# Two heads' products in a fixed order, another emission pace, and neighbourhood scores that no longer wait for the values

## The chip, the cores and the metric

The kernel runs on one core of one Trainium2 chip. The metric is device time in microseconds (us), from the start to the end of the one launch. The five engines of the core are written as in the profile: PE (TensorE, matrix products; PEld is its weight load), DVE (VectorE), ACT (ScalarE), POOL (GpSimd, which here only issues transfers) and SP (SyncE, transfers too).

## The reference, cut to what matters

A trunk of two layers over 512 tokens of width 1024. Each layer is a half-step feed-forward block, a mixer, and a second half-step feed-forward block; a last RMSNorm closes the trunk.

```python
x = x + 0.5 * swiglu(rmsnorm(x, ffn1_norm), ffn1_wg, ffn1_wu, ffn1_wd)
h = rmsnorm(x, mix_norm)
proj = h @ w_in            # q, k, v of 8 neighbourhood heads; q, k, v, gate, codes of 4 GLA heads
na_o  = rmsnorm(neighbourhood_attention(q, k, v, rpb), na_gain)
o_fwd = gla_chunked(qg, kg, vg, log_gf, True)
o_bwd = flip(gla_chunked(flip(qg), flip(kg), flip(vg), flip(log_gb), False))
gla_o = rmsnorm(o_fwd + o_bwd, gla_gain) * silu(g_r)
x = x + concatenate([na_o, gla_o], axis=-1) @ w_out
x = x + 0.5 * swiglu(rmsnorm(x, ffn2_norm), ffn2_wg, ffn2_wu, ffn2_wd)
```

Only the mixer is touched by the change. Everything is in float32.

## The kernel before

**Products.** A large product is done in three passes (`mm3`, L168): each operand is split into a high part and a rest (`split`, L147: ACT writes the high part, DVE the rest), and high*high, high*rest, rest*high are summed in PSUM. The weights arrive by DMA, are split into tiles `wh` and `wl` (six buffers each), and PE takes 512 columns a time. The small products of the attention are plain float32; the trace shows each of them as two records.

**The mixer** (`mixer`, L533) has four streams of work:

- `fillers` (L930) walks through `PAIRS`: eleven pairs of 128-wide column blocks of the input projection, one after the other. A pair takes 48 products of 512 columns (96 of 256 for the values `v`), and its `post` writes the scaled result. After the last pair come the output projection's products over the four neighbourhood head pairs (`op_part(c, 0, 4)`), which the generator emits once the neighbourhood part is normalised, then those over the gated linear attention (GLA) heads.
- `na_all` (L901) runs eight units (`na_unit`, L842), each half the queries of two heads: scores (L853), softmax (L860 to L871), transposes (L876), products with the values (L887). Three units are in flight, at different ages.
- `gla_all(0)`, `gla_all(1)` (L970) each treat two GLA heads: decay factors, then scores by levels of a binary tree of block sizes. Eight sets of 64x64 blocks (`blocks`, L624), one of 128x128 blocks (L701), two of 128x256 (L715), and at last `gla_out` (L753), which sums the products with the values.

The two heads of a unit lie in SBUF rows 0 to 63 and 64 to 127, so their score products use different halves of PE's rows; the two heads' products with the values use different halves of its columns. The kernel emits head 0, head 1, head 0, head 1.

**What sets the order.** `interleave` (L505) decides in which order the four streams emit. Each stream yields pairs (time its work takes, time until it should go on); the stream that is ready emits. `LVL` is the pause of a GLA stream after a level's DVE work, `NAP` the length of a neighbourhood unit, `OUTT` the time booked for a `gla_out`. A stream that yields a name waits until that result exists in `got`. The emission order is then handed to the tile framework, which makes each engine's final order from it by its own estimate of times, subject to the data and to the buffers. On the chip each engine takes its instructions in that final order.

**Buffers.** PSUM has eight banks: four `mm` (projections, GLA outputs, output projection), two `sc` (all scores, always taken as a pair), one `tp` (transposes and norm sums), one `o` (products of the neighbourhood heads with the values). So only one set of scores exists at a time, and the next waits until DVE or ACT has read the one before.

**Names.** The trace and the orders cut buffer numbers or layer digits from names: `M_mm` a projection or output product, `M_sc` scores, `M_tp` a transpose, `M_o` products with the values, `M_pp` the probabilities, `M_ga` and `M_kt` the GLA operands, `M_at`, `M_am`, `M_af` GLA score matrices, `M_vt` scaled GLA values before their transposes, `M_gv` after, `M_nacc` the sum of squares of the neighbourhood output, `M_oh` split outputs, `M_r` a reciprocal root.

Of the kernel before, what the change touches and what calls it, by code (L numbers as in the profile page):

```python
# [15 lines left out]
P = 128  # L16
# [8 lines left out]
LVL = 8.71  # L25
# [8 lines left out]
NAP = 10.4  # L34
# [24 lines left out]
OUTT = 8.24  # L59
# [4 lines left out]
def trunk_kernel(ctx, tc, xin, wgu, wdn, win, wcode, wgate, wout, vec, rpbt,  # L64
# [102 lines left out]

    def mm3(ps, wh, wl, rh, rl, first, last, more=False):  # L168
        PE.matmul(ps, wh, rh, start=first, stop=False, skip_group_check=more)  # L169
        PE.matmul(ps, wh, rl, start=False, stop=False, skip_group_check=more)  # L170
        PE.matmul(ps, wl, rh, start=False, stop=last, skip_group_check=more)  # L171

# [360 lines left out]
    def mixer(l):  # L533
        st["lab"] = f"M{l}"
        got = {}
# [63 lines left out]
        def gla_levels(pr):  # L599
# [24 lines left out]
            def blocks(pss, op):  # L624


                for i in range(8):
                    o = (i % 2) * 64
                    for hh in range(2):
                        PE.matmul(pss[hh][o:o + 64, (i // 2) * 64:(i // 2 + 1) * 64], *op(hh, i),  # L630
                                  start=True, stop=True)
# [17 lines left out]
            for li, h in enumerate((1, 2, 4, 8, 16, 32, 64, 128)):  # L649
# [45 lines left out]
                elif h2 == 128:  # L695
                    pss = psum("sc"), psum("sc")
                    for s in range(4):
                        t = s ^ 1
                        kk, qq = (KF, QF) if s < t else (KB, QB)
                        for hh in range(2):  # L700
                            PE.matmul(pss[hh][:, s * P:(s + 1) * P], kk[rows[hh], s * P:(s + 1) * P],  # L701
                                      qq[rows[hh], t * P:(t + 1) * P], start=True, stop=True)
# [4 lines left out]
                else:  # L707
                    for half in range(2):
# [3 lines left out]
                        for j in range(2):  # L712
                            s = 2 * half + j
                            for hh in range(2):
                                PE.matmul(pss[hh][:, j * 256:(j + 1) * 256],  # L715
                                          kk[rows[hh], s * P:(s + 1) * P], qq[rows[hh], o:o + 256],
                                          start=True, stop=True)
# [124 lines left out]
        def na_unit(hp, jp, pps, ctxd):  # L842
# [4 lines left out]
            for jj in range(2):  # L847
                j = 2 * jp + jj
                for hh in range(2):
                    kb = k[rows[hh], :]  # L850
                    krhs = bass.AP(kb.tensor, kb.offset + KOFF[j][0],
                                   [list(kb.ap[0]), [64, 2], [KOFF[j][1], 2], [1, 64]])
                    PE.matmul(sco[hh][:, jj * 256:(jj + 1) * 256], q[rows[hh], j * P:(j + 1) * P], krhs,  # L853
                              start=True, stop=True)
# [24 lines left out]
            if jp == 0:  # L879
                ctxd["po"] = psum("o")  # L880
            po = ctxd["po"]
            for jj in range(2):
                j = 2 * jp + jj
                for c in range(2):
                    v = got["v", hp][VSEL[j][c]]
                    for hh in range(2):
                        PE.matmul(po[rows[hh], j * P:(j + 1) * P], v[:, rows[hh]],  # L887
                                  pps[hh][:, (jj * 2 + c) * P:(jj * 2 + c + 1) * P],
                                  start=(c == 0), stop=(c == 1))
# [11 lines left out]
        def na_all():  # L901
# [4 lines left out]
            for u in range(8 + DEEP):  # L906
                if u < 8:
                    yield ("qk", u // 2)
                    yield ("v", u // 2)
                    units.append(na_unit(u // 2, u % 2, pps, ctxd))  # L910
                left = NAP if u < 8 else 3.0
                for age, n in enumerate((1, 2, 1)):
                    if 0 <= u - age < 8:
                        for _ in range(n):
                            y = next(units[u - age])
                            left -= sum(y)
                            yield y
# [233 lines left out]
```

## Time and profile before

| | us |
|---|---|
| median of 3 runs (lowest to highest) | 1954.99 (1954.86 to 1955.47) |
| the profiled execution | 1957.23 |
| its span, first to last instruction | 1955.5 |
| layer 0: start of the mixer to the start of the attention | 361.5 to 386.0 |
| layer 0: attention beside the projections | 386.0 to 548.7 |
| layer 0: attention after the last projection product | 548.7 to 562.8 |
| layer 0: GLA outputs and most of the output projection | 562.8 to 617.1 |
| layer 0: rest of the output projection | 617.1 to 634.4 |
| layer 1: the same mixer | 1328.5 to 1597.4 |

The rest of the span is the four feed-forward blocks. The profile page gives busy time for each engine, the chain of work that ended last, and groups of equal instructions. The mean granted clock of TensorE is 0.991 of full speed over the span. A table by stretches gives busy time and granted clock of each stage; the timeline gives start and length of single instructions. Products overlap in PE's pipeline, so the length of one record is longer than the time to the next; what a product costs is read from start to start.

### The profile page before, as it was taken

What the parts mean: (1) busy time and instruction counts of PE and PEld (TensorE: products, weight loads), DVE (VectorE), ACT (ScalarE), POOL (GpSimd) and SP (SyncE); (2) the same over time, 40 slices, a digit from 0 to 9 for tenths busy, and PEclk for the clock granted to TensorE, in tenths of its full rate; (3) what the DMA queues carried; (4) which work ended last, traced back from release to release, by engine and by line L of the source; (5) the groups of instructions that cost most, each with busy time, mean ns of one, the idle gap of its engine ahead of it and who ended that gap; (6) DMA issues with size and microseconds to landing.
All of it is one profiled execution on the core that took longest, in us unless ns stands there. A gap on an engine that the chain in (4) does not pass through costs nothing.

```text
span 1955.5 us, 32220 instructions
## 1 busy us (share of the span) xinstructions
PE 1924.7 (98%) x12490; PEld 1687.4 (86%) x12490; DVE 1416.9 (72%) x2705; ACT 1020.1 (52%) x1959; POOL 17.4 (1%) x36
## 2 busy tenths in 40 slices
PE   8999999999998999999999999999999999999997
PEld 7889989888777898999889899988887778999896
DVE  6958768676558875967788596776764689679585
ACT  5535536465564553644555364455654655546364
POOL 0000000000000000000000000000000000000000
PEclk9999999999999999999999999999999899999999
DMA  4333223322202332332223333232221033233322
GB/s 154 112 108 108 89 106 124 110 67 98 66 31 85 102 108 89 106 108 103 83 98 106 108 109 107 88 119 96 96 86 55 21 120 107 89 107 109 108 76 76
DMA packets 58249, 187.78 MB, mean 96 GB/s; under 512 B 6640, under 2 KB 13296, under 8 KB 45808
## 3 DMA queue, kind: packets, MB, share of 16 engines
q1 hardware_dynamic: 29904, 132.07, 19.8%
q10 hardware_dynamic: 25632, 45.27, 7.0%
q0 software_dynamic: 2560, 8.39, 1.3%
q8 instruction: 98, 1.61, 0.3%
q14 instruction: 55, 0.45, 0.1%
HBM read 183.60 MB, written 2.10 MB: 95 GB/s over the span
## 4 chain that ended last, share of the span: by engine, by line
PE 97%; DVE 1%; DMA 1%; ACT 1%; issue 0%; DVEq 0%; ACTq 0%
PE F_mm L169 14%; PE F_mm L171 14%; PE F_mm L170 14%; PE F_sc L169 9%; PE F_sc L170 9%; PE F_sc L171 9%; PE M_mm L169 6%; PE M_mm L170 6%; PE M_mm L171 6%; PE M_o L887 1%; PE M_sc L630 1%; PE M_tp L876 1%; PE M_sc L853 1%; PE M_mm L773 1%; PE M_sc L715 1%; DMA wraw<-in_wgu 0%
## 5 line engine op out<-in xcount | busy, mean ns | idle before, releaser
L149 ACT ACTIVATE F_wh<-F_wraw 128x512 fp32r<-128x512 f32 (+1 forms) x472 | 289.5, 617 | 439.9 <-PE F_sc L170 238.8
L169 PE MATMUL F_mm<-F_xc,F_wh 128*128 128x256 f32 x1792 | 500.5, 282 | 1.3 <-ACT F_wh L149 1.3
L170 PE MATMUL F_mm<-F_xc,F_wh 128*128 128x256 f32 x1792 | 501.5, 282 | 0.0
L171 PE MATMUL F_mm<-F_xc,F_wl 128*128 128x256 f32 x1792 | 495.2, 282 | 0.0
L150 DVE TENSOR_TENSOR F_wl<-F_wraw,F_wh 128x512 fp32r<-128x512 f32 (+1 forms) x472 | 312.8, 668 | 151.9 <-ACT F_wh L149 143.4
L169 PEld LDWEIGHTS F_mm<-F_xc,F_wh 128*128 128x128 f32 x1792 | 339.3, 190 | 3.7 <-ACT F_wh L149 1.9
L170 PEld LDWEIGHTS F_mm<-F_xc,F_wh 128*128 128x128 f32 x1792 | 340.3, 190 | 1.9
L171 PEld LDWEIGHTS F_mm<-F_xc,F_wl 128*128 128x128 f32 x1792 | 335.8, 190 | 0.0
L169 PE MATMUL F_sc<-F_hid,F_wh 128*128 128x512 f32 (+1 forms) x716 | 275.6, 387 | 1.3 <-DVE xt L455 1.3
L170 PE MATMUL F_sc<-F_hid,F_wh 128*128 128x512 f32 (+1 forms) x716 | 276.6, 386 | 0.0
L171 PE MATMUL F_sc<-F_hid,F_wl 128*128 128x512 f32 (+1 forms) x716 | 276.4, 386 | 0.0
L149 ACT ACTIVATE F_wh<-F_ws 128x512 fp32r<-128x512 f32 x256 | 161.8, 632 | 170.0 <-PE F_mm L170 109.8
L150 DVE TENSOR_TENSOR F_wl<-F_ws,F_wh 128x512 fp32r<-128x512 f32 x256 | 174.8, 688 | 41.8 <-ACT F_wh L149 38.8
L169 PEld LDWEIGHTS F_sc<-F_hid,F_wh 128*128 128x128 f32 x716 | 134.6, 188 | 29.0 <-DVE xt L455 3.0
L171 PEld LDWEIGHTS F_sc<-F_hid,F_wl 128*128 128x128 f32 x716 | 134.5, 188 | 26.4
L170 PEld LDWEIGHTS F_sc<-F_hid,F_wh 128*128 128x128 f32 x716 | 134.6, 188 | 25.7
L455 DVE SCALAR_TENSOR_TENSOR xt<-F_sc,xt 128x512 f32<-128x512 f32 x94 | 65.0, 691 | 96.7 <-PE F_sc L171 96.1
L169 PE MATMUL M_mm<-F_xd,M_wh 128*128 128x512 f32 x304 | 122.1, 403 | 0.0
L171 PE MATMUL M_mm<-F_xd,M_wl 128*128 128x512 f32 x304 | 120.3, 397 | 0.0
L170 PE MATMUL M_mm<-F_xd,M_wh 128*128 128x512 f32 x304 | 119.9, 395 | 0.0
L150 DVE TENSOR_TENSOR M_wl<-M_wraw,M_wh 128x512 fp32r<-128x512 f32 (+1 forms) x112 | 73.4, 669 | 35.9 <-ACT M_wh L149 32.4
L149 ACT ACTIVATE M_wh<-M_wraw 128x512 fp32r<-128x512 f32 (+1 forms) x112 | 67.6, 614 | 46.8 <-PE M_mm L170 37.9
(325 smaller groups left out, 3153.0 us busy)
## 6 DMA issues: line engine op xcount, KB each, us to landing
F_wraw<-in_wgu SPq DMA_DIRECT2D x64, 1024.0 KB, 4.7
F_wraw<-in_wdn SPq DMA_DIRECT2D x32, 1024.0 KB, 4.9
M_wraw<-in_win ACTq DMA_DIRECT2D x88, 256.0 KB, 3.6
F_wraw<-in_wgu ACTq DMA_DIRECT2D x80, 256.0 KB, 3.8
F_wraw<-in_wdn SPq DMA_DIRECT2D x16, 768.0 KB, 4.3
M_pp<-in_rpbt POOLq DMA_DIRECT2D x32, 256.0 KB, 3.1
M_wraw<-in_wout SPq DMA_DIRECT2D x16, 256.0 KB, 2.7
xt<-in_xin SPq DMA_DIRECT2D x8, 256.0 KB, 5.2
```

Source lines behind the costliest of these rows:

```text
L149: S.activation(h, src, AF.Copy)
L150: V.tensor_tensor(l, src, h.bitcast(F32), op=ALU.subtract)
L169: PE.matmul(ps, wh, rh, start=first, stop=False, skip_group_check=more)
L170: PE.matmul(ps, wh, rl, start=False, stop=False, skip_group_check=more)
L171: PE.matmul(ps, wl, rh, start=False, stop=last, skip_group_check=more)
L455: V.scalar_tensor_tensor(xt[:, c, :], pss[j], 0.5, xt[:, c, :], ALU.mult, ALU.add)
L630: PE.matmul(pss[hh][o:o + 64, (i // 2) * 64:(i // 2 + 1) * 64], *op(hh, i), start=True, stop=True)
L715: PE.matmul(pss[hh][:, j * 256:(j + 1) * 256], kk[rows[hh], s * P:(s + 1) * P], qq[rows[hh], o:o + 256], start=True, stop=True)
L773: PE.matmul(dst, vs(2 * half + j), fa[:, o:o + P], start=False, stop=(j == 1))
L853: PE.matmul(sco[hh][:, jj * 256:(jj + 1) * 256], q[rows[hh], j * P:(j + 1) * P], krhs, start=True, stop=True)
L876: PE.transpose(pt[:, i * P:(i + 1) * P], pp[:, i * P:(i + 1) * P], idn)
L887: PE.matmul(po[rows[hh], j * P:(j + 1) * P], v[:, rows[hh]], pps[hh][:, (jj * 2 + c) * P:(jj * 2 + c + 1) * P], start=(c == 0), stop=(c == 1))
```

## The change

**The head pairs.** A new helper `paired` takes a list of products and emits them in that order; all but the first of a list are told to stay in program order. Five places use it: the 64x64, 128x128 and 128x256 scores of the GLA streams, and the scores and the products with the values of the neighbourhood units. Within a pair head 1 now comes before head 0. The number, shape and operands of the products are the same.

**The pace.** `LVL` goes from 8.71 to 5.0, `NAP` from 10.4 to 8.0, `OUTT` from 8.24 to 3.6.

**The wait for the values.** A neighbourhood unit used to be created when both its queries and keys (`qk`) and its values (`v`) existed. Now it starts with `qk` alone, and the stream waits for `v` only before the products with the values.

```diff
-LVL = 8.71
+LVL = 5.0
-NAP = 10.4
+NAP = 8.0
-OUTT = 8.24
+OUTT = 3.6
...
+    def paired(mms):
+
+        for i, (ps, lhs, rhs, kw) in enumerate(mms):
+            ins = PE.matmul(ps, lhs, rhs, **kw)
+            if i:
+                tc.keep_in_program_order(ins)
+
...
-                for i in range(8):
-                    o = (i % 2) * 64
-                    for hh in range(2):
-                        PE.matmul(pss[hh][o:o + 64, (i // 2) * 64:(i // 2 + 1) * 64], *op(hh, i),
-                                  start=True, stop=True)
+                paired([(pss[hh][i % 2 * 64:i % 2 * 64 + 64, (i // 2) * 64:(i // 2 + 1) * 64], *op(hh, i), SS)
+                        for i in range(8) for hh in (1, 0)])
...
             if jp == 0:
+                yield ("v", hp)
                 ctxd["po"] = psum("o")
...
             for u in range(8 + DEEP):
                 if u < 8:
                     yield ("qk", u // 2)
-                    yield ("v", u // 2)
                     units.append(na_unit(u // 2, u % 2, pps, ctxd))
...
                             y = next(units[u - age])
+                            if isinstance(y[0], str):
+                                yield y
+                                y = next(units[u - age])
```

The final order of every engine in both mixers differs from the one before; the feed-forward blocks keep theirs but for a few rows at the start of the second one. In layer 0 (layer 1 has the same order in both versions) these are the places to know. In the orders of the changed kernel the products of `paired` stand under its line, L171, and the three passes of `mm3` under L176 to L178.

*Place 1: PE, the first set of 128x256 scores of a GLA stream, before.*

```order
L170 MATMUL M_mm_5645<-F_xd_3834,M_wh_5667 128x512
L715 MATMUL M_sc_5529<-M_ga_4147 128x256 x2
L171 MATMUL M_mm_5645<-F_xd_3834,M_wl_5668 128x512
L715 MATMUL M_sc_5530<-M_ga_4147 128x256 x2
L169 MATMUL M_mm_5800<-F_xd_3605,M_wh_5802 128x512
```

*The second set of the same stream in the changed kernel:*

```order
L176 MATMUL M_mm_5729<-F_xd_3681,M_wh_5761 128x512
L171 MATMUL M_sc_5268<-M_ga_4165 128x256
L177 MATMUL M_mm_5729<-F_xd_3681,M_wh_5761 128x512
L171 MATMUL M_sc_5267<-M_ga_4165 128x256
L171 MATMUL M_sc_5268<-M_ga_4165 128x256
L171 MATMUL M_sc_5267<-M_ga_4165 128x256
L178 MATMUL M_mm_5729<-F_xd_3681,M_wl_5762 128x512
```

Before, both products of head 0 (`M_sc_5529`) stand together, and those of head 1 behind a projection product. Now the heads alternate, but the first product, which is not held in order, stands alone ahead of a projection product.

*Place 2: PE at the last projection product of the mixer, before.* `M_mm_5800` and `M_mm_5801` are the last projection pair.

```order
L170 MATMUL M_mm_5801<-F_xd_3834,M_wh_5823 128x512
L171 MATMUL M_mm_5801<-F_xd_3834,M_wl_5824 128x512
L630 MATMUL M_sc_5700<-M_ga_4630 64x64 x8
L630 MATMUL M_sc_5701<-M_ga_4630 64x64 x8
L876 MATMUL M_tp_5734<-con,M_pp_5501 128x128 x4
L701 MATMUL M_sc_5865<-M_ga_4630 128x128 x4
L701 MATMUL M_sc_5866<-M_ga_4630 128x128 x4
L876 MATMUL M_tp_5750<-con,M_pp_5503 128x128 x4
L887 MATMUL M_o_5762<-M_pp_5501,M_vm_4993 64x128
L715 MATMUL M_sc_6005<-M_ga_4630 128x256 x2
```

Behind the last projection product stand one set of 64x64 scores, the transposes of the last neighbourhood unit (its scores are long done), and the 128x128 and 128x256 scores.

*The same place in the changed kernel, two pieces.* `M_mm_5854` and `M_mm_5855` are the last projection pair.

```order
L177 MATMUL M_mm_5855<-F_xd_3834,M_wh_5877 128x512
L178 MATMUL M_mm_5855<-F_xd_3834,M_wl_5878 128x512
L881 MATMUL M_tp_5525<-con,M_pp_5168 128x128 x4
L171 MATMUL M_sc_5466<-M_ga_4804,M_kt_5416 64x64
L171 MATMUL M_sc_5465<-M_ga_4804,M_kt_5416 64x64
```

```order
L171 MATMUL M_o_5655<-M_pp_5166,M_vm_5213 64x128
L171 MATMUL M_sc_5486<-M_k_5334,M_q_5333 128x256
L171 MATMUL M_sc_5485<-M_k_5334,M_q_5333 128x256
L171 MATMUL M_sc_5486<-M_k_5334,M_q_5333 128x256
L171 MATMUL M_sc_5485<-M_k_5334,M_q_5333 128x256
L171 MATMUL M_sc_5565<-M_ga_4804 64x64
```

Now two sets of 64x64 scores, the products of unit 6 with its values, and the scores of the last unit (`M_k`, `M_q`) themselves stand behind the last projection product. After them come, as before, its transposes, the 128x128 scores, and the 128x256 scores.

*Place 3: DVE around the end of the neighbourhood part, before.* `M_vt_5777` and `M_vt_5778` are the values of two GLA heads on their way to their transposes.

```order
L727 TENSOR_TENSOR M_vt_5777<-M_mm_5644,M_r_3913 128x8x8x8
L727 TENSOR_TENSOR M_vt_5778<-M_mm_5645,M_r_3913 128x8x8x8
L150 TENSOR_TENSOR M_wl_6201<-M_wraw_6198,M_wh_6200 128x512
L666 TENSOR_TENSOR M_ga_4630<-M_ga_4630,M_pk_4494 128x4x64
L667 TENSOR_TENSOR M_ga_4630<-M_ga_4630,M_pk_4515 128x4x64
```

*The same values in the changed kernel:*

```order
L899 TENSOR_TENSOR M_nacc_4629<-M_nacc_4629,M_sq_5695 128x512
L150 TENSOR_TENSOR M_sql_5747<-M_nacc_4629,M_sqh_5746 128x512
L256 TENSOR_SCALAR M_ms_5752<-M_tp_5745 128x512
L257 TENSOR_TENSOR M_a_5754<-M_r_5753 128x512
L258 SCALAR_TENSOR_TENSOR M_a_5754<-M_a_5754,M_ms_5752 128x512
L259 SCALAR_TENSOR_TENSOR M_r_5753<-M_a_5754,M_r_5753 128x512
L731 TENSOR_TENSOR M_vt_5845<-M_mm_5729,M_r_3913 128x8x8x8
L731 TENSOR_TENSOR M_vt_5846<-M_mm_5730,M_r_3913 128x8x8x8
```

Before, the values are scaled ahead of the last levels of the GLA stream. Now they stand behind the whole normalisation of the neighbourhood output, and on PE their transposes and the GLA outputs (L773 and on) stand behind that too.

## Rows read from the trace of the kernel before

**Rows 1.** The page, part 1: busy time of each engine.

```profile
PE 1924.7 (98%) x12490; PEld 1687.4 (86%) x12490; DVE 1416.9 (72%) x2705; ACT 1020.1 (52%) x1959; POOL 17.4 (1%) x36
```

**Rows 2.** Stretches (length, busy of each engine, clock, DMA): layer 0, then layer 1.

```profile
386.00:548.70 162.70, 162.70 (x1350) 128.12 (x1348) 105.38 (x310) 91.17 (x207) 5.35 (x10) 1.00 0.24 79
548.70:562.80 14.10, 12.04 (x97) 8.99 (x97) 4.93 (x12) 9.01 (x19) 0.00 (x0) 0.76 0.11 39
562.80:617.10 54.30, 51.28 (x285) 44.31 (x284) 41.13 (x70) 26.27 (x47) 0.00 (x0) 0.97 0.12 40
617.10:634.40 17.30, 14.79 (x57) 11.49 (x56) 15.61 (x26) 12.98 (x22) 0.00 (x0) 0.90 0.35 116
...
1583.00:1597.40 14.40, 13.30 (x57) 10.35 (x56) 14.20 (x24) 12.16 (x21) 0.00 (x0) 1.00 0.31 99
```

**Rows 3.** What PE waited for: total us, times, longest, both layers.

```profile
PE M_mm L169 <- ACT M_on L777: 6.0, 2, 3.0
...
PE M_sc L701 <- ACT M_at L693: 3.5, 3, 1.6
PE OP_mm L171 <- DVE OP_wl L150: 2.6, 2, 2.3
```

**Rows 4.** Timeline of PE (start, length, instruction): a lone product with the values.

```profile
498.95 0.39 PE L170 MATMUL M_mm<-F_xd,M_wh 128*128 128x512 f32 x1
499.18 0.40 PE L171 MATMUL M_mm<-F_xd,M_wl 128*128 128x512 f32 x1
499.51 0.43 PE L887 MATMUL M_o<-M_pp,M_v 128*64 128x128 f32 x2
499.87 0.50 PE L171 MATMUL M_mm<-F_xd,M_wl 128*128 128x512 f32 x1
500.20 0.39 PE L169 MATMUL M_mm<-F_xd,M_wh 128*128 128x512 f32 x1
```

**Rows 5.** Timeline of PE: 128x256 products, alternating, by head, and split by head.

```profile
413.85 1.13 PE L853 MATMUL M_sc<-M_k,M_q 64*128 64x256 f32 x8
...
463.84 1.14 PE L853 MATMUL M_sc<-M_k,M_q 64*128 64x256 f32 x8
...
526.94 1.13 PE L715 MATMUL M_sc<-M_ga 64*128 64x256 f32 x4
528.00 0.50 PE L171 MATMUL M_mm<-F_xd,M_wl 128*128 128x512 f32 x1
528.43 1.13 PE L715 MATMUL M_sc<-M_ga 64*128 64x256 f32 x4
```

**Rows 6.** Timeline of PE, DVE and ACT around the last projection product, layer 0.

```profile
539.48 1.14 PE L853 MATMUL M_sc<-M_k,M_q 64*128 64x256 f32 x8
...
542.23 0.51 ACT L865 ACTIVATE M_pp<-M_pp,M_sm 128x256 f32<-128x256 f32 x1 [0.39 <-DVE M_sm L863]
...
544.54 0.62 DVE L871 TENSOR_SCALAR M_pp<-M_pp,M_sm 128x256 f32<-128x256 f32 x2
...
551.01 0.75 ACT L693 ACTIVATE M_at<-M_sc 64x256 f32<-64x256 f32 x2
...
551.81 1.16 PE L701 MATMUL M_sc<-M_ga 64*128 64x128 f32 x8 [1.56 <-ACT M_at L693]
...
556.53 2.09 PE L715 MATMUL M_sc<-M_ga 64*128 64x256 f32 x8
```

**Rows 7.** Stretches before, in and after the clock's falls, layer 0.

```profile
550.70:554.10 3.40, 1.79 (x13) 1.60 (x14) 1.42 (x4) 3.29 (x9) 0.00 (x0) 1.00 0.44 151
554.10:561.00 6.90, 6.90 (x36) 4.88 (x35) 1.43 (x4) 3.15 (x6) 0.00 (x0) 0.51 0.00 2
...
591.70:595.10 3.40, 3.40 (x10) 2.62 (x9) 3.40 (x7) 0.42 (x1) 0.00 (x0) 0.50 0.00 0
```

**Rows 8.** Groups (count, busy, mean ns, idle before): full-width steps of ACT, DVE.

```profile
L152 ACT ACTIVATE M_oh<-M_o,vecs 128x512 fp32r<-128x512 f32 x4 | 2.8, 689 | 12.4 <-PE M_o L887 12.4
...
L898 DVE TENSOR_TENSOR M_nacc<-M_nacc,M_sq 128x512 f32<-128x512 f32 x3 | 2.1, 688 | 0.7 <-ACT M_sq L897 0.7
```

More of the change, by code (lines that the diff above doesn't have):

```diff
@@ L171, in mm3 @@
         PE.matmul(ps, wl, rh, start=False, stop=last, skip_group_check=more)
+    SS = dict(start=True, stop=True)
     XC = [None] * KP
@@ L696, in gla_levels @@
                     pss = psum("sc"), psum("sc")
+                    mms = []
                     for s in range(4):
@@ L699, in gla_levels @@
                         kk, qq = (KF, QF) if s < t else (KB, QB)
-                        for hh in range(2):
-                            PE.matmul(pss[hh][:, s * P:(s + 1) * P], kk[rows[hh], s * P:(s + 1) * P],
-                                      qq[rows[hh], t * P:(t + 1) * P], start=True, stop=True)
+                        mms += [(pss[hh][:, s * P:(s + 1) * P], kk[rows[hh], s * P:(s + 1) * P],
+                                 qq[rows[hh], t * P:(t + 1) * P], SS) for hh in (1, 0)]
+                    paired(mms)
                     for hh in range(2):
@@ L711, in gla_levels @@
                         o = 256 * (1 - half)
[L712 to L717, printed above, removed]
+                        paired([(pss[hh][:, j * 256:(j + 1) * 256],
+                                 kk[rows[hh], (2 * half + j) * P:(2 * half + j + 1) * P], qq[rows[hh], o:o + 256], SS)
+                                for j in range(2) for hh in (1, 0)])
                         for hh in range(2):
@@ L846, in na_unit, with keys @@
             rows = slice(0, 64), slice(64, P)
[L847 to L854, printed above, removed]
+            def keys(hh, j):
+                kb = k[rows[hh], :]
+                return bass.AP(kb.tensor, kb.offset + KOFF[j][0],
+                               [list(kb.ap[0]), [64, 2], [KOFF[j][1], 2], [1, 64]])
+            paired([(sco[hh][:, jj * 256:(jj + 1) * 256],
+                     q[rows[hh], (2 * jp + jj) * P:(2 * jp + jj + 1) * P], keys(hh, 2 * jp + jj), SS)
+                    for jj in range(2) for hh in (1, 0)])
             halves = slice(0, H2), slice(H2, T)
@@ L879, in na_unit @@
             if jp == 0:
+                yield ("v", hp)
                 ctxd["po"] = psum("o")
             po = ctxd["po"]
[L882 to L889, printed above, removed]
+            paired([(po[rows[hh], j * P:(j + 1) * P], got["v", hp][VSEL[j][c]][:, rows[hh]],
+                     pps[hh][:, (j % 2 * 2 + c) * P:(j % 2 * 2 + c + 1) * P], dict(start=c == 0, stop=c == 1))
+                    for j in (2 * jp, 2 * jp + 1) for c in range(2) for hh in (1, 0)])
             if jp == 1:
```

## The prediction

> **What bounds the kernel now.** I read the page first: PE is busy for 1924.7 us of a span of 1955.5 [rows 1], so time can only come from PE's idle time, from its slow clock, or from products that take less. The change reorders the two mixers alone, so I went on to the table by stretches [rows 2]. From 386.0 to 548.7, where the attention runs beside the projections, PE is busy for the whole 162.7 us at full clock: there is no wait to remove there, and only cheaper products could shorten it. The losses lie behind the last projection product, in three pieces per layer. In the 14.1 us after it PE idles 2.1 us and its clock is 0.76. In the 54.3 us of GLA outputs and output projection it idles 3.0 us at clock 0.97. In the last 17.3 us it idles 2.5 us at clock 0.90. The list of waits names them [rows 3]: PE waits for ACT's copies of GLA scores (L693, 3.5 us in both layers), for ACT's copies of GLA outputs (L777, 6.0) and for a weight split on DVE (2.6). Each is followed by a fall of the clock: with 1.8 us of PE work in the 3.4 us from 550.7, the next 6.9 us run at 0.51, the lower of its two levels, 1.2 GHz [rows 7]. So what the change does to the work behind the last projection product counts most.
>
> **The pairs.** The rows price a small product by what it adds between two big ones. Big ones of 512 columns follow each other at 0.23 us (498.95 to 499.18); a lone product with the values starts 0.33 after the big one ahead, the next big one 0.36 later, the one after that 0.33 later [rows 4]: 1.02 where two steps of 0.23 stood, 0.57 us for the lone product. So much is a visit to the small tiles for the least work; the trace has none of a single 64x64 product. Four alternating 128x256 products last 1.13 us; the same four in the order head 0, head 0, head 1, head 1 last 1.14 [rows 5]: as long as they stand together, their order hardly matters. Torn apart by a big product they last 1.13 for one head and 1.13 again for the other [rows 5], a whole visit more, 1.3 us with its entry and exit.
>
> So pinning pays where a pair was torn, and costs where the first product, which is not pinned, now stands alone. Going through PE's order of layer 0: the change heals two torn 256-column sets (1.3 us each) and three lone products with the values (0.57 each), 4.3 us. It makes eight lone first products of 64x64 sets, which I put at 0.45 us, since they stream half the columns of the lone one seen; four wider ones at 0.6 to 0.8; and tears three runs of products with the values: 7.5 us. Runs that now touch each other, and 64x64 sets that took up to 1.0 us for the 0.8 of a regular one, give back 3.5. In sum all small products of the mixer take 50.9 us before (waits and slow clock taken off) and 50.6 after, 0.3 us less a layer. I take that, by the price of the lone product with the values, the nearest row; both ends go into the range: 0.1 us if a lone 64x64 product's entry merges with that of its set two products later, 0.57 if it costs as much as the one seen.
>
> A page of the Trainium skill, "TensorE: Matmul & The Clock Gate" (Part 3: Packing small matmuls), says that matmuls start and end strictly in program order and only weight loads are pulled ahead. By that rule the order by heads would leave the first and the last product without a partner, and alternation would save about 0.45 us in each such set. The rows speak against it: 1.14 against 1.13 us [rows 5].
>
> **What ends up behind the last projection product.** Ahead of it the small work is 2.8 us shorter after the change (43.6 us in 40 runs from start to start between 386.0 and 548.7 before; 42.2 by the prices above after, less four transposes that come, plus two groups of value transposes that go). So the last projection product comes 2.8 us earlier. But what left has gone behind it: one more set of 64x64 scores, unit 6's products, unit 7's scores, the value transposes. These form a chain, and no projection product is left to lie beside it. From the last projection product, with durations of the trace:
>
> 1. Transposes 0.5, 64x64 scores 0.8, unit 6's products 1.2, nearly back to back: unit 7's scores start at 2.55 and end at 3.8.
> 2. The next 64x64 set needs the two score banks. In the trace the scores start at 539.48 and ACT's first exponential, which follows DVE's reading of both, at 542.23: 2.75 later [rows 6]. So 5.2 to 6.0; PE idles 1.4.
> 3. Unit 7's first transposes need its first head's probabilities. The second head's start being weighted at 544.54, the first's were done about 0.4 earlier, 4.7 after the scores [rows 6]: 7.25 to 7.8, idle 1.25.
> 4. The 128x128 scores need the banks back from ACT's copies at L693, 0.38 each (two in 0.75, [rows 6]); six of eight stand behind the exponentials in ACT's order: 7.25 and 2.4 make 9.65, idle 1.85.
> 5. PE has then worked 3.4 of the last 7.1 us, as little as ahead of the fall at 554.1 [rows 7], so I put the next stretch at the low level: 128x128 scores 1.8, transposes 1.1, 128x256 scores 2.1 (2.09 in such a stretch, twice the 1.13 at full clock; [rows 5, 6]), products 1.9, second 128x256 scores 1.4. That ends at 17.9, the products at 16.5.
> 6. Unit 7's output, then its normalisation, on ACT and DVE in turn: two ACT steps, the sum of squares on DVE, ACT's and DVE's split, PE 0.5, logarithm and exponential, three DVE steps, then the first GLA value. Eleven steps at 0.6 to 0.69 [rows 8] and PE's: 24.0. Two groups of value transposes, each with an ACT copy between: the GLA outputs start at 25.8. Before, the values had been scaled ahead of all this, and they start 14.1 us after the last projection product [rows 2].
>
> The GLA outputs thus start 25.8 - 14.1 - 2.8 = 8.9 us later than before.
>
> **What comes back.** Behind that point the stretch of 54.3 us holds 3.0 us of idle time, 1.7 of slow clock (3.4 us at 0.50, [rows 7]) and 0.5 of norm products that are now done. The fourth GLA output stands earlier among the output products, so I expect no such wait for ACT: 49.1 us of PE work. But it begins after 7.9 us in which PE worked 2.6, so half clock for up to 6.9 us again, as from 554.1: at most 3.4 lost, I take 2.5. So 51.6 instead of 54.3, 2.7 back. A layer loses 8.9 - 2.7 = 6.2 us, two layers 12.4. In the last stretch layer 0 loses 2.5 us of idle time and 1.7 of clock, layer 1 1.1 and nothing [rows 2]; with the normalisation already off DVE I take 1.1 for both, a gain of 3.1. Sum: 12.4 - 3.1 = +9.3 us on the profiled execution's 1957.2, 1966.5; the median of the runs lies 2.2 below that execution, so **1964**.
>
> **The rivals.**
>
> *It cancels* (1951 to 1959). The chain is shorter than worked out: ACT and DVE have little else there, and if the clock holds through step 5 (3.5 us less) a layer ends up 2.7 us later; with the 3.1 from the last stretch that is +2.3, 1957. For it speaks that ACT is busy for only 9.0 of 14.1 us there [rows 2]; against it, that before one wait of 1.56 us was enough for the fall.
>
> *Faster, by lone first products that cost nothing* (1944). If a lone 64x64 product costs 0.1 us and not 0.45, and the other four 0.35 less, a layer saves 4.2 us; with the clock held as well (3.5 and 2.5) it changes by 6.2 - 6.0 - 4.2 = -4.0, and the sum by 2 x -4.0 - 3.1 = -11. With a held clock alone the sum is -2.7, no change; it turns faster once the twelve lone products cost 0.6 us a layer less than put here. Against it: the one kind of lone product seen does cost 0.57 [rows 4], and the clock fell after less idling than now [rows 7].
>
> *Much slower* (1976). DVE becomes the bound behind the chain: four normalisations of GLA outputs, some seven steps of 0.6 each, and sixteen output steps and the weight splits stand in a row; before, DVE was the one that PE's last wait led to [rows 3]. If the last GLA output comes 3 us late in each layer and the clock falls again (1.7), that is 9.4 us more, and the 3.1 of the last stretch don't come.
>
> *Program order on PE is strict* (1959). By the rule above five sets a layer that stood by heads would gain about 0.5 us each, 5 us in all. Rows 5 leave little of it.
>
> *The pairs don't hold* is no case of its own: the order shows them, and shows that the first product is loose.
>
> **How the numbers follow.** Forecast 0.53, cancel 0.16, faster 0.13, much slower 0.15, strict order 0.03. Runs of this kernel agree within about 0.03%, so 0.2%, 3.9 us, is what I count as no change: 1951.1 to 1958.9. Faster is the one case, 0.14 with the lower end of the second; the same 0.17 with a little of the forecast; slower 0.69. The range leaves out most of the fast case and the end of the slow one: 1950 to 1976.
>
> **What would show it.** Right: the stretch ahead of the last projection product stays without idle time; between it and the first GLA output lie about 26 us with PE idle for more than 8 and a clock well below 1; PE waits there for DVE and ACT (scores before the transposes, copies before the 128x128 scores, the scaled values before their transposes); the wait for L777 is gone. Lone 64x64 products cost near 0.45 us. Wrong would be a stretch of 18 us or less there, a full clock through it, or small products that sum to clearly less than 50 us a layer.

## The result, and the profile after the change

The changed kernel takes 1970.77 us (median of four runs, 1968.99 to 1972.84), the kernel before 1954.92 in the same comparison. The ratio is 1.0086, with a 95% interval of 1.0071 to 1.0101: slower by some 16 us. The page's first part, beside [rows 1]:

```profile
PE 1931.8 (98%) x12490; PEld 1691.3 (86%) x12490; DVE 1415.1 (72%) x2705; ACT 1018.8 (52%) x1959; POOL 17.3 (1%) x36
```

PE has the same 12490 records and is busy 7.1 us longer, though no product was added: a sign of more work at the low clock. The span is 1971.1, 15.6 more than before. The table by stretches (us, length, busy time of PE, PEld, DVE, ACT and POOL with their instructions, granted clock, DMA share, GB/s); the first four rows are layer 0 and answer to [rows 2], the last two are layer 1:

```profile
386.80:546.90 160.10, 160.10 (x1280) 125.30 (x1279) 98.48 (x288) 86.26 (x194) 5.32 (x10) 1.00 0.24 78
546.90:566.40 19.50, 13.57 (x150) 9.98 (x148) 10.05 (x34) 11.99 (x29) 0.00 (x0) 0.82 0.12 41
566.40:575.40 9.00, 5.20 (x18) 3.38 (x19) 5.76 (x9) 3.98 (x7) 0.00 (x0) 0.63 0.00 0
575.40:640.40 65.00, 63.91 (x337) 54.90 (x337) 50.68 (x85) 36.55 (x63) 0.00 (x0) 0.97 0.19 61
...
1518.40:1547.90 29.50, 19.56 (x168) 13.84 (x167) 15.72 (x42) 15.97 (x35) 0.00 (x0) 0.72 0.09 27
1547.90:1613.00 65.10, 64.04 (x337) 55.04 (x337) 50.71 (x85) 36.55 (x63) 0.00 (x0) 0.97 0.19 61
```

The attention beside the projections is 2.6 us shorter (160.1 against 162.7) and still without idle time. Between the last projection product and the GLA outputs lie 28.5 us in layer 0 and 29.5 in layer 1 ("the chain" from here on); before, 14.1 and 13.1. PE works 18.8 and 19.6 of them, at a clock of 0.82, 0.63 and 0.72. What follows is shorter, 65.0 against 54.3 + 17.3 = 71.6 in layer 0, and 65.1 against 68.7 in layer 1. These are layer 1's chain and what follows it in the kernel before:

```profile
1515.60:1528.70 13.10, 11.68 (x97) 8.81 (x97) 5.06 (x12) 9.10 (x19) 0.00 (x0) 0.74 0.14 43
1528.70:1597.40 68.70, 64.58 (x340) 54.63 (x339) 55.21 (x93) 38.73 (x68) 0.00 (x0) 0.98 0.18 57
```

The list of PE's waits of the changed kernel (total us, times, longest, both layers), where [rows 3] had the GLA outputs' copies on top:

```profile
PE M_tp L245 <- ACT M_sqh L149: 5.0, 2, 2.5
...
PE M_tp L737 <- ACT M_gv L739: 4.1, 6, 0.7
PE M_tp L737 <- DVE M_ms L256: 3.0, 2, 1.5
PE M_sc L171 <- DVE M_sm L865: 2.6, 4, 1.0
PE M_tp L881 <- DVE M_pp L876: 2.4, 2, 1.3
```

The wait for the GLA outputs is gone. In its place PE waits for the norm of the neighbourhood output (ACT's split `M_sqh` ahead of its sum on PE, DVE's mean square `M_ms` behind it) and for ACT's copies between the value transposes (`M_gv`), 12.1 of the 17.1 us shown. The timeline of PE in layer 0 from the last projection product (start, length, instruction, idle time before it) shows the chain:

```profile
546.69 0.40 PE L178 MATMUL M_mm<-F_xd,M_wl 128*128 128x512 f32 x1
...
549.57 1.13 PE L171 MATMUL M_sc<-M_k,M_q 64*128 64x256 f32 x8
551.60 0.33 PE L171 MATMUL M_sc<-M_ga 64*64 64x64 f32 x2 [0.90 <-DVE M_sm L865]
...
554.09 0.70 PE L881 MATMUL M_tp<-con,M_pp 128*128 128x128 f32 x4 [1.11 <-DVE M_pp L876]
...
556.23 2.07 PE L171 MATMUL M_sc<-M_ga 64*128 64x128 f32 x14 [0.31 <-ACT M_at L699]
...
562.70 1.16 PE L171 MATMUL M_sc<-M_ga 64*128 64x256 f32 x8
566.36 0.49 PE L245 MATMUL M_tp<-M_sqh,onr 128*128 128x512 f32 x1 [2.50 <-ACT M_sqh L149]
...
569.09 1.11 PE L737 MATMUL M_tp<-con,M_vt 128*128 128x128 f32 x4 [1.50 <-DVE M_ms L256]
570.89 1.12 PE L737 MATMUL M_tp<-con,M_vt 128*128 128x128 f32 x4 [0.69 <-ACT M_gv L739]
...
575.40 0.63 PE L773 MATMUL M_mm<-M_at,M_gv 128*128 128x128 f32 x2
```

Four groups of value transposes stand behind the norm, 1.80 apart, at the low clock (1.11 us for a group; the last one of the kernel before, at full clock, took 0.66). In sum by stretches, layer 0 and layer 1, from start to start of the products that bound them: ahead -2.5 and -2.5, the chain +14.3 and +16.3, what follows -6.6 and -3.6: +15.5 unrounded, and 0.1 elsewhere. By the rows, half of the chain's growth is idle time of PE (9.7 and 9.9 us against 2.1 and 1.4); the rest is work that moved there, and the low clock.

### The profile page after: what moved, and what is told of

The parts are those of the page before. It is cut to its first block, busy times and chain, and to the rows that moved or that the text cites. A ratio compares the mean times of both kernels' runs of the same rounds, so it can differ in the third digit from the quotient of the medians.

```text
span 1971.1 us, 32200 instructions
## 1 busy us (share of the span) xinstructions
PE 1931.8 (98%) x12490; PEld 1691.3 (86%) x12490; DVE 1415.1 (72%) x2705; ACT 1018.8 (52%) x1959; POOL 17.3 (1%) x36
## 3 DMA queue, kind: packets, MB, share of 16 engines
q1 hardware_dynamic: 29904, 132.07, 19.6%
## 4 chain that ended last, share of the span: by engine, by line
PE 96%; DVE 2%; ACT 1%; DMA 1%; issue 0%; DVEq 0%; ACTq 0%
PE F_mm L176 14%; PE F_mm L178 14%; PE F_mm L177 14%; PE F_sc L176 9%; PE F_sc L177 9%; PE F_sc L178 9%; PE M_mm L176 6%; PE M_mm L177 6%; PE M_mm L178 5%; PE M_sc L171 3%; PE M_o L171 1%; PE M_mm L777 1%; PE M_tp L881 1%; PE M_tp L737 0%; DMA wraw<-in_wgu 0%
## 5 line engine op out<-in xcount | busy, mean ns | idle before, releaser
L176 PE MATMUL F_mm<-F_xc,F_wh 128*128 128x256 f32 x1792 | 500.2, 282 | 0.9 <-ACT F_wh L149 0.9
L178 PE MATMUL F_mm<-F_xc,F_wl 128*128 128x256 f32 x1792 | 495.5, 282 | 0.0
L176 PEld LDWEIGHTS F_mm<-F_xc,F_wh 128*128 128x128 f32 x1792 | 339.3, 190 | 3.1 <-ACT F_wh L149 1.3
L178 PEld LDWEIGHTS F_mm<-F_xc,F_wl 128*128 128x128 f32 x1792 | 335.9, 190 | 0.0
L176 PE MATMUL F_sc<-F_hid,F_wh 128*128 128x512 f32 (+1 forms) x716 | 275.6, 387 | 1.3 <-DVE xt L464 1.3
L178 PE MATMUL F_sc<-F_hid,F_wl 128*128 128x512 f32 (+1 forms) x716 | 276.4, 386 | 0.0
L176 PEld LDWEIGHTS F_sc<-F_hid,F_wh 128*128 128x128 f32 x716 | 134.5, 188 | 28.9 <-DVE xt L464 3.0
L178 PEld LDWEIGHTS F_sc<-F_hid,F_wl 128*128 128x128 f32 x716 | 134.5, 188 | 26.6
L176 PE MATMUL M_mm<-F_xd,M_wh 128*128 128x512 f32 x304 | 122.6, 403 | 0.0
L178 PE MATMUL M_mm<-F_xd,M_wl 128*128 128x512 f32 x304 | 118.7, 395 | 0.0
```

## The experiments

Theory "drain": the loss comes from what the order puts behind the last projection product, where PE waits and runs slow; and of that, above all, from the norm standing ahead of the value transposes. Rivals: the pairs themselves, by their loose first products; values that DVE and ACT scale late in any case; and order by heads (both products of one head, then both of the other) being dear on PE. Each kernel is compared with the kernel before on the same chip (1954.91 for the first four, 1955.68 for the next four, 1954.81 for the last four).

### The three parts alone

The pairs alone: the changed kernel with the old numbers and the old place of the wait.

```diff
-LVL = 5.0
+LVL = 8.71
-NAP = 8.0
+NAP = 10.4
-OUTT = 3.6
+OUTT = 8.24
...
                     yield ("qk", u // 2)
+                    yield ("v", u // 2)
...
-                yield ("v", hp)
                 ctxd["po"] = psum("o")
```

> The head pairs alone, with the old pace and the old wait for the values. Theory 'drain' (what counts is what stands behind the last projection product, not the pairs): in the order the small products ahead of the last projection product come to 3.7 us less a layer by the prices of the prediction, and a chain of some 20 us stands behind it instead of 14.1 and 13.1, of which the later output products give back about 4; so 1950 to 1958, no clear loss. Rival 'lone firsts' (the loose first products and the alternation are what costs): most of the loss of 15.8 us is here already, 1965 to 1971.

Measured: 1950.21, ratio 0.9979 (0.9969 to 0.9989). There is no loss: the pairs alone gain 4.7 us, with the pins (the calls that hold a product in program order) included.

The pace alone: the kernel before with the three new numbers.

```diff
-LVL = 8.71
+LVL = 5.0
-NAP = 10.4
+NAP = 8.0
-OUTT = 8.24
+OUTT = 3.6
```

> The three pace numbers alone; heads emitted as before, nothing pinned, old wait for the values. Theory 'drain': most of the loss is here. Ahead of the last projection product 3.2 us less a layer; behind it scores of the last unit, transposes, 128 and 256 sets, the norm, then the value transposes, some 26 us instead of 14.1 and 13.1; 5 us come back in the output products: 1960 to 1968. Rival 'lone firsts': no new lone first products, so no loss, 1953 to 1957.

Measured: 1965.95, ratio 1.0051 (1.0032 to 1.0070). The pace brings 11.0 of the 15.9 us. Its timeline behind the last projection product (546.82) ends in the same way, with two groups of value transposes behind the norm:

```profile
568.63 0.80 PE L236 MATMUL M_tp<-M_sqh,onr 128*128 128x512 f32 x1 [2.09 <-ACT M_sqh L149]
...
571.72 1.12 PE L733 MATMUL M_tp<-con,M_vt 128*128 128x128 f32 x4 [1.56 <-DVE M_ms L247]
573.52 1.11 PE L733 MATMUL M_tp<-con,M_vt 128*128 128x128 f32 x4 [0.69 <-ACT M_gv L735]
574.43 0.64 PE L769 MATMUL M_mm<-M_at,M_gv 128*128 128x128 f32 x2
```

The chain is 27.4 us long in layer 0 and 27.3 in layer 1.

The later wait alone: the kernel before, with `yield ("v", hp)` ahead of the products with the values.

```diff
-                    yield ("v", u // 2)
...
             if jp == 0:
+                yield ("v", hp)
```

> The later wait for the values alone. In the order nothing at all stands between the last projection product and the GLA outputs, and the small products ahead of it come to 9.7 us more a layer. Theory 'drain': 9.7 us more ahead, 13.6 us less behind, some 4 us a layer: 1943 to 1952, faster than before. Rival 'nothing in it': the same work only stands elsewhere, 1953 to 1958.

Measured: 1942.95, ratio 0.9934 (0.9919 to 0.9949): 12.0 us faster, at the lower edge of the range. The GLA outputs of the first two heads now start at 555.10, beside the projections. Two stretches of layer 0, the attention beside the projections and the 11 us from the last projection product to the outputs of the other two heads:

```profile
388.50:566.40 177.90, 177.90 (x1480) 140.31 (x1479) 110.33 (x322) 101.69 (x226) 5.45 (x10) 1.00 0.20 67
566.40:577.40 11.00, 11.00 (x55) 8.21 (x53) 9.60 (x17) 9.54 (x16) 0.00 (x0) 1.00 0.29 96
```

There is no idle time and the clock is full: all of the attention but two sets of 128x256 scores has gone ahead (177.9 us from the first score, against 159.5 before), and what fills the 11 us around these sets are output and norm products. So one of the three parts alone gains about as much as another alone costs.

### The norm in a bank of its own

The numbers in the tile names count the order in which the code asks for them. In the changed kernel the norm's bank is `M_tp_5745`, and the value transposes come later, 5775 to 5891; before, the transposes were 5674 to 5837 and the norm 5879. There is one bank for all of them, given out in that order. This kernel takes the norm's sums from the bank of the products with the values instead, which is free by then.

```diff
-        ps = psum("tp")
+        ps = psum("o" if tag == "na" else "tp")
```

> The changed kernel, with the norm sums of the neighbourhood output put into the bank of its products instead of the one transpose bank. Theory 'bank order' (the transpose bank is handed out in the order of emission; at the new pace the norm is emitted ahead of the value transposes, so they wait for the whole normalisation): the transposes move ahead of the norm, GLA outputs start 20 to 22 us behind the last projection product instead of 28.5 and 29.4, 1955 to 1962. Rival 'DVE and ACT are late anyway' (the scaled values come late for their own reasons): within 3 us of the changed kernel, 1968 to 1974.

Measured: 1958.19, ratio 1.0014 (1.0005 to 1.0024); 12.6 of the 15.9 us are gone. Its timeline of PE, layer 0, last projection product at 543.58:

```profile
558.95 0.66 PE L737 MATMUL M_tp<-con,M_vt 128*128 128x128 f32 x4
559.54 1.13 PE L171 MATMUL M_sc<-M_ga 64*128 64x256 f32 x8
560.61 0.66 PE L737 MATMUL M_tp<-con,M_vt 128*128 128x128 f32 x4
562.80 0.49 PE L245 MATMUL M_o<-M_sqh,onr 128*128 128x512 f32 x1 [1.54 <-ACT M_sqh L149]
563.29 0.66 PE L737 MATMUL M_tp<-con,M_vt 128*128 128x128 f32 x4
...
565.54 0.63 PE L773 MATMUL M_mm<-M_at,M_gv 128*128 128x128 f32 x2
```

The transposes now lie beside the last scores and between the norm's two products, and none of them waits for the norm's logarithm and mean square, the two steps that read its sums out of the bank. The stretch ahead is as long as in the changed kernel, 157.0 from the first score; the chain is 21.7 and 23.8 instead of 28.5 and 29.4, 12.4 us less for both layers. The two profiled executions lie 17.2 us apart, more than the medians: 1.7 of the rest are in what follows the chain, and 3.1 ahead of the first mixer, which the edit doesn't touch. So it was the bank, not DVE or ACT being late. The other waits of the chain stay.

### The parts in pairs, and the pins

The changed kernel without its pins (same order of emission, nothing held):

```diff
             ins = PE.matmul(ps, lhs, rhs, **kw)
-            if i:
+            if False:
                 tc.keep_in_program_order(ins)
```

> The changed kernel with the same emission (head 1 ahead of head 0, new pace, later wait) but no product held in program order. By the order, ahead of the last projection product stand 35 runs of small products instead of 45 and 4 lone ones instead of 16; by the prices of the prediction 3.6 us less a layer; what stands behind is nearly the same, norm and four groups of value transposes included. Theory 'lone firsts cost what the lone products with the values do': the attention beside the projections 3 to 4 us shorter than the 157.0 of the changed kernel, the chain behind as long, 1961 to 1967. Rival 'a lone first product merges with its set and costs nothing': 156 to 157.5 there, 1968 to 1973. Rival 'strict order on PE' (sets that go back to order by heads lose 0.5 us each): as long or longer, 1970 to 1975.

Measured: 1964.42, ratio 1.0050 (1.0035 to 1.0065), 6.4 us less than the changed kernel. From the first score to the last projection product it takes 152.3 against 157.0, 4.6 less, somewhat more than expected; the chain behind, 30.0 and 30.7, is 1.5 and 1.3 longer than with pins. So the pins cost, and the long chain isn't theirs.

The changed kernel with the old pace (pairs and later wait):

```diff
-LVL = 5.0
+LVL = 8.71
-NAP = 8.0
+NAP = 10.4
-OUTT = 3.6
+OUTT = 8.24
```

> The changed kernel with the old pace: pairs and the later wait for the values. If the parts simply add (pairs -4.6 us, later wait -11.9): 1937 to 1940. Theory 'drain': the pins put a 64x64 set, the 128 set and the 256 sets behind the last projection product again, where with the later wait alone stood nothing; ahead of it 5.9 us less a layer by the prices, behind it a chain of some 8 to 10 us with waits and a low clock: 1942 to 1952.

Measured: 1949.75, ratio 0.9972 (0.9962 to 0.9982). The parts don't add, which would have made 1937 to 1940. By the table of stretches a chain of 11.1 and 11.9 us is back behind the last projection product, with PE idle for 4.1 and 3.8 of it, where the later wait alone had none.

The later wait, head 1 first, no pins, old pace (the kernel of the last experiment without pins):

```diff
-            if i:
+            if False:
                 tc.keep_in_program_order(ins)
```

> The kernel before with the later wait for the values and head 1 emitted ahead of head 0 in every set, nothing pinned, old pace. In the order 45.1 us of small products stand ahead of the last projection product by the prices (44.3 before, 54.0 with the later wait alone) and behind it only a group of transposes, the 128 set and another group, and no norm. Theory 'drain': behind it some 5 us instead of 14.1 and 13.1: 1934 to 1943, at least as fast as the later wait alone. Rival 'order by heads is dear, so the pins are needed': slower than pairs with the later wait.

Measured: 1932.76, ratio 0.9885 (0.9870 to 0.9900), 22.9 us faster than before and 17.0 faster than the same with pins, 1.2 under the range. The GLA outputs start 3.4 us behind the last projection product.

The changed kernel without the pairs (new pace, later wait; the products in the code of the kernel before):

```diff
-            paired([(sco[hh][:, jj * 256:(jj + 1) * 256],
...
+                    PE.matmul(sco[hh][:, jj * 256:(jj + 1) * 256], q[rows[hh], j * P:(j + 1) * P], krhs,
+                              start=True, stop=True)
```

> The changed kernel without the pairs: new pace and later wait, products emitted and ordered as before. In the order behind the last projection product stand products with the values, both 256 sets, the norm and then all four groups of value transposes. Theory 'drain' with 'bank order': the scores have gone ahead (6 us more there than with the pace alone), but the norm still stands ahead of the transposes, 16 to 20 us behind instead of 27.3: 1954 to 1964. If the parts simply add (pace +11.0, later wait -11.9): 1954. If the pace's loss were the scores of the last unit alone and not the norm: 1945 or less.

Measured: 1954.89, ratio 0.9998 (0.9988 to 1.0007). That rules out the third sum of the expectation (1945 or less). The other two both reach it, so the total doesn't tell them apart; the timeline speaks for the norm. The scores of the last unit have gone ahead, yet the norm's products and all four groups of transposes, 1.80 apart at the low clock, still end a chain of 15.8 us in layer 0 and 16.0 in layer 1:

```profile
556.82 0.80 PE L236 MATMUL M_tp<-M_sqh,onr 128*128 128x512 f32 x1 [0.23 <-ACT M_sqh L149]
...
559.85 1.11 PE L733 MATMUL M_tp<-con,M_vt 128*128 128x128 f32 x4 [1.51 <-DVE M_ms L247]
561.65 1.11 PE L733 MATMUL M_tp<-con,M_vt 128*128 128x128 f32 x4 [0.69 <-ACT M_gv L735]
...
566.17 0.63 PE L769 MATMUL M_mm<-M_at,M_gv 128*128 128x128 f32 x2
```

### What a pin costs

The pairs alone without their pins: the first kernel of this section, and in it again

```diff
-            if i:
+            if False:
                 tc.keep_in_program_order(ins)
```

> The pairs without their pins: head 1 emitted ahead of head 0 in every set, nothing held in order; old pace, old wait for the values. In the order the same things stand behind the last projection product as with the pairs alone; ahead of it 31 runs of small products instead of 41, 4 of them lone instead of 15. So this against the pairs alone is the price of the pins. Theory 'a lone first product costs about 0.5 us': the attention beside the projections 4.5 to 5.5 us shorter than the 155.5 of the pairs alone, the chain behind it equal to 0.5 us, 1939 to 1942. Rival 'alternation pays what the lone products cost': 155 to 156 there, 1949 to 1952.

Measured: 1939.91, ratio 0.9922 (0.9907 to 0.9937), 10.3 us below the same with pins. The attention beside the projections, layer 0, of the pinned kernel (first row, with its chain) and of this one, which has the same 1255 records:

```profile
386.90:542.40 155.50, 155.50 (x1255) 121.91 (x1253) 96.00 (x283) 85.09 (x189) 5.32 (x10) 1.00 0.23 76
542.40:558.70 16.30, 13.66 (x166) 9.93 (x166) 10.47 (x33) 12.63 (x30) 0.00 (x0) 1.00 0.21 64
```

```profile
387.70:536.95 149.25, 149.25 (x1255) 119.55 (x1253) 96.10 (x283) 85.56 (x189) 5.32 (x10) 1.00 0.24 79
536.95:553.55 16.60, 14.12 (x166) 10.68 (x166) 10.56 (x33) 12.62 (x30) 0.00 (x0) 1.00 0.19 64
```

That is 6.25 us less, more than the 4.5 to 5.5 expected, for eleven lone first products fewer in each layer: 0.57 each in the mean, if all of it is theirs. The chain is equal to 0.3 us. So the rival by which alternation pays for the lone products falls.

The eleven are not alike: seven are 64x64 products, three 128x256 and one 128x128. The trace of the changed kernel has both main kinds:

```profile
430.75 0.40 PE L177 MATMUL M_mm<-F_xd,M_wh 128*128 128x512 f32 x1
431.08 0.32 PE L171 MATMUL M_sc<-M_ga,M_kt 64*64 64x64 f32 x2
431.33 0.49 PE L178 MATMUL M_mm<-F_xd,M_wl 128*128 128x512 f32 x1
431.76 0.69 PE L171 MATMUL M_sc<-M_ga,M_kt 64*64 64x64 f32 x30
...
523.27 0.39 PE L176 MATMUL M_mm<-F_xd,M_wh 128*128 128x512 f32 x1
523.59 0.70 PE L171 MATMUL M_sc<-M_ga 64*128 64x256 f32 x2
524.21 0.50 PE L177 MATMUL M_mm<-F_xd,M_wh 128*128 128x512 f32 x1
524.64 1.13 PE L171 MATMUL M_sc<-M_ga 64*128 64x256 f32 x6
```

From the projection product ahead of the lone one to the rest of its set it takes 1.01 and 1.37 us. Without the lone product that is a step of 0.23 and an entry of 0.33 into the set, 0.56; so a lone 64x64 product costs 0.45 and a lone 128x256 product 0.81. Seven and three at these prices, and the 128x128 one at 0.6 (517.64 in the kernel with pins), make 6.2 us, about the 6.25 measured.

In this kernel three sets of neighbourhood scores a layer still stand by heads; the timeline has such a set at 465.06 and an alternating one at 424.77:

```profile
424.77 1.13 PE L171 MATMUL M_sc<-M_k,M_q 64*128 64x256 f32 x8
...
465.06 1.14 PE L171 MATMUL M_sc<-M_k,M_q 64*128 64x256 f32 x8
```

1.14 by heads, 1.13 alternating: the same as [rows 5]. There two products of one head, of the same shape, take 1.13 alone, so the two heads run at the same time even where PE's order has one behind the other. The rule of the Trainium skill, "TensorE: Matmul & The Clock Gate" (Part 3: Packing small matmuls), that matmuls start and end strictly in program order does not show in these sets. Against the kernel before this one is 14.9 us faster: what the pairs gain comes from emitting head 1 first, and the pins take 10.3 of it away.

### The last cell, and two kernels that try for more

The changed kernel with the old wait (pairs and pace):

```diff
                     yield ("qk", u // 2)
+                    yield ("v", u // 2)
...
-                yield ("v", hp)
                 ctxd["po"] = psum("o")
```

> The changed kernel with the old wait for the values: pairs and new pace. If the parts add (pairs -4.6, pace +11.0): 1961. Theory 'drain' with 'bank order': in the order the scores of the last unit, the 128 and 256 sets and two groups of value transposes stand ahead of the norm, the norm and two groups of transposes behind it; a chain of 25 to 28 us as with the pace alone, and ahead of it about as much: 1960 to 1969.

Measured: 1966.55, ratio 1.0058 (1.0043 to 1.0073): no better than the pace alone; the pairs' gain is lost. The chain is 25.9 and 26.1 us long. The whole table, each against its kernel before, in us:

| | old wait | later wait |
|---|---|---|
| old pace, no pairs | 0 | -12.0 |
| old pace, pairs | -4.7 | -5.9 |
| new pace, no pairs | +11.0 | -0.8 |
| new pace, pairs | +11.7 | +15.9 |

The later wait is worth 12 us without the pairs at either pace; with the pairs and the new pace it costs 4. The new pace costs 11 to 22 everywhere. The pairs gain 4.7 in the kernel before, and cost 16.7 beside the other two parts: there they shorten the stretch ahead by 5.0 us a layer (157.0 against 162.0) and lengthen the chain by 12.7 and 13.4.

The later wait and head 1 first, nothing pinned, with a slower pace of the levels:

```diff
-LVL = 8.71
+LVL = 10.0
-NAP = 10.4
+NAP = 9.2
```

> The later wait and head 1 first, nothing pinned, with LVL 10.0 and NAP 9.2. In the order nothing stands between the last projection product and the GLA outputs; 2.4 us more ahead of it a layer by the prices, against 3.4 us (1.1 of them idle) behind it with the old pace: no more than 2 us from 1932.8 by theory 'drain', 1930 to 1936. Rival 'the clock's falls behind it are the rest of the loss': below 1930.

Measured: 1937.38 (1933.72 to 1937.95), ratio 0.9905 (0.9890 to 0.9920), outside the range by 1.4 us. As expected the GLA outputs follow the last projection product by 1.6 us without idle time, but in what follows PE idles 3.2 us a layer, against 0.8 to 0.9 with the old pace: the wait has moved on. No gain was left in that place.

The later wait and head 1 first, nothing pinned, a shorter unit and the norm in its own bank:

```diff
-NAP = 10.4
+NAP = 9.2
...
-        ps = psum("tp")
+        ps = psum("o" if tag == "na" else "tp")
```

> The later wait and head 1 first, nothing pinned, LVL 8.71, NAP 9.2, and the norm of the neighbourhood output in the bank of its products. In the order only the 128 set and one group of transposes stand behind the last projection product; ahead of it 0.6 us more by the prices. Theory 'drain': 1930 to 1936, the same as with the old pace. Rival 'the own bank is worth its 13 us here too': 1925 or less, which theory 'drain' rules out, since no norm stands ahead of the transposes with the old pace.

Measured: 1928.65 (1928.02 to 1929.33), ratio 0.9863 (0.9847 to 0.9880): the fastest here, 26.2 us below the kernel before and 42 below the changed one. It lies 1.4 us under the range of "drain" and 3.7 above what the rival asked for. Its stretches in layer 0, the attention, the chain and what follows:

```profile
388.80:549.80 161.00, 161.00 (x1394) 127.73 (x1392) 105.00 (x314) 95.75 (x216) 5.33 (x10) 1.00 0.22 73
549.80:551.40 1.60, 1.60 (x22) 1.48 (x22) 0.93 (x2) 1.54 (x3) 0.00 (x0) 1.00 0.00 0
551.40:617.60 66.20, 65.50 (x354) 54.64 (x353) 54.34 (x93) 40.63 (x70) 0.00 (x0) 1.00 0.23 71
```

PE is idle 0.7 us in 228.8, at full clock. Which of its two edits took the last 3 to 4 us against 1932.76 was not tried. The reason given for ruling the rival out doesn't hold: in that kernel the norm's first product (547.10) does stand ahead of the last two groups of value transposes (550.24 and 553.18), so a part of the gain can be the bank's.

## Why the prediction was right, and where its sum fell short

The direction was right, and the time lies in the range, 6.8 us above the forecast of 1964. By its steps:

- **Ahead of the last projection product.** Forecast 2.8 us earlier a layer, measured 2.5, without idle time. Right, and its prices too: 0.45 was put in for a lone 64x64 product and 0.6 to 0.8 for a wider one, and the trace shows 0.45 and 0.81. The 0.57 of the kernels with and without pins is the mean of both kinds, and not the upper bound of the 64x64 product come true.
- **Steps 1 to 4 of the chain.** From 546.92: the last unit's scores at 2.65 (forecast 2.55), the 64x64 set from 4.7 to 6.1 (5.2 to 6.0), its transposes at 7.2 (7.25), the bulk of the 128x128 scores at 9.3 (9.65). Right, and by the waits named: DVE's reading of the scores, the probabilities, ACT's copies.
- **Step 5.** The clock fell near where it was put (0.70 in the 3.4 us from 553.7, 0.50 in the next), and the second 128x256 scores end at 16.9 instead of 17.9. Right, though one sum is not: with its own waits of 1.4, 1.25 and 1.85 us PE would have worked 2.6 of the 7.1 us ahead, not 3.4. In the trace it worked 3.63 of the 6.66 from 549.57.
- **Step 6, the norm.** Value transposes can start at 22.2 in layer 0 and 23.1 in layer 1; forecast 24.0. The time is nearly right, the wait is another: not for values scaled behind the norm, but for the bank, until `M_ms` has read the sums (DVE, 568.34 to 569.03). The first two heads' values had been scaled from 516.8 on; only the other two's are scaled behind the norm, from 571.06.
- **Step 6, the value transposes: wrong.** "Two groups of value transposes, each with an ACT copy between", 1.8 us. There are four groups, and the clock has fallen once more: 1.11 for a group and 0.69 of waiting for ACT's copy, 6.3 us (569.09 to 575.40), 4.5 more than put in, in each layer. Before, two of the four groups had gone through by then. In the order of PE the four groups could be counted; the step took over the picture of the kernel before, where two stand late. What keeps them there is the bank: the prediction had the values behind the norm on DVE, but not why the transposes are.
- **Layer 1.** The forecast took layer 0's 14.1 us for both layers. Layer 1 had 13.1, another 1.0.
- **What comes back.** Forecast 2 x 2.7 + 3.1 = 8.5, measured 10.1: the wait for L777 is gone, as named, and the low clock lasts from 575.4 to about 578.8, so that 1.7 us were lost and not the 2.5 put in.

So the 6.2 us between 15.5 and 9.3 are 9.0 for the transposes and 1.0 for layer 1, less 1.8 and 0.9 for the norm's earlier end and 1.6 for what comes back, with 0.5 more ahead.

Of the rivals, *it cancels* fell with the length of the chain. *Lone first products that cost nothing* fell by the kernels without pins. *Much slower* came near the time for another reason: PE idles 1.1 us a layer behind the GLA outputs, so DVE is not the bound there. *Strict order* finds nothing to gain in the sets by heads.

Against the whole, what the prediction took for one mechanism has three. The pace moves work behind the projections and puts the norm ahead of the transposes, of whose cost the one bank makes 12.6 us. The pins cost 6 to 17 us, by lone products and by what they move. And the order of emission by itself, head 1 first and nothing pinned, gains 14.9 us in the kernel before and 11.0 beside the later wait, but costs 9.5 beside the later wait and the new pace: there it takes 9.7 us a layer from the stretch ahead (152.3 against 162.0) and adds 14.1 and 14.7 to the chain. The later wait gains 12 us without the pairs. Why it turns to a loss with both others is answered in part only: at the new pace all four groups of value transposes stand behind the norm with it and two with the old wait, and that order is what the bank's 12.6 us hang on; but no run changes this alone beside the old wait.

## What to carry to other kernels

Small dependent work that lies free beside large products costs its whole chain once the products have run out, and here it cost more again in clock: look at what the order puts behind the last large product before counting what each piece costs ahead of it. Where one buffer serves two chains, it is the order of asking that decides: a long chain that asks first makes the short one wait, and another buffer can be worth more than the reordering. Hold a set together whole or not at all: sets with the first product left loose were torn in eleven places a layer here, at 0.45 us for a 64x64 product and 0.81 for a 128x256 one. And an edit that gains alone can cost beside others, since each moves the whole order: read the stretches of the kernel that it goes into.

## What the runs showed of the hardware

Idle time in small pieces didn't always bring the clock down. The chain of the pairs alone has 2.6 us of idle time in 16.3, in pieces of at most 1.04, and its row above shows a clock of 1.00; so does the same chain without pins, with 2.5 in 16.6. In the changed kernel PE idled 5.9 of the first 19.5 us of the chain, at 0.82. It worked 1.42 of the 3.4 us ahead of the first fall, and in the next 3.4 the granted clock was 0.70 (the lower of the two levels, 1.2 GHz, for a part of them):

```profile
550.30:553.70 3.40, 1.42 (x36) 0.74 (x32) 2.33 (x13) 1.91 (x7) 0.00 (x0) 1.00 0.34 120
553.70:557.10 3.40, 2.35 (x14) 1.77 (x16) 2.62 (x9) 3.30 (x11) 0.00 (x0) 0.70 0.02 5
```
